# A build-time clock that orders a kernel's instructions gets measured durations and finer dependencies

## The chip, the cores and the metric

The kernel runs on one core of one Trainium2 chip. The metric is the device time of one execution in microseconds, the median of several runs; less is better. A core has TensorE (PE, with its weight loads as PEld), VectorE (DVE), ScalarE (ACT), GpSimd (POOL) and SyncE (SP, which here only issues DMAs). Each takes its instructions strictly in the order in which they stand in its queue, and semaphores order the engines among each other.

## What is computed

Two blocks in float32 on one sequence of 256 positions and 2048 channels, each with a modulation from a condition vector `c`, a mixer and a feed-forward part:

```
mod = silu(c) @ w_ada + b_ada
sh_m, sc_m, gt_m, sh_f, sc_f, gt_f = split(mod, 6)
h = rmsnorm(x) * (1 + sc_m) + sh_m
proj = h @ w_in
y = concat(hgrn2(proj), gated_delta(proj)) @ w_out     # block 1
x = x + gt_m * rmsnorm(y)
h = rmsnorm(x) * (1 + sc_f) + sh_f
y = square(relu(h @ w_ff1)) @ w_ff2                    # block 1
x = x + gt_f * rmsnorm(y)
```

The second block has the same frame; its mixer is four kinds of attention side by side (with a forgetting gate, "fox"; compressed, selected and windowed, "nsa"; dilated, "dil"; the difference of two softmaxes, "diff"), and its feed-forward part is a gated one, `(silu(u @ w_gate) * (u @ w_up)) @ w_down`. The gated delta rule solves a unit lower triangular system of 64 by 64 for each chunk and head:

```
m = where(strict, beta * (k @ k.T) * gamma, 0)
sol = triangular_solve(eye + m, [v * beta, k * beta * exp(g)])
```

## The kernel before

All weights stream once from HBM, 512 KB to a DMA on SP's queue, into a ring of `raw` buffers. A product keeps float32's precision by splitting: ScalarE copies a raw tile to a rounded high part (`wh<-raw`), VectorE or GpSimd subtracts to get the low part (`wl<-raw,wh`), and TensorE adds three products, x high with w high, x high with w low, x low with w high, into a PSUM bank `g`. The split activations are `hT`, and `rh`, `rl` or `o2h`, `o2l` further on. A split weight tile is called a unit here; there are four slots for `wh` and `wl`, sometimes six. The other large stream is that of the modulation weights (`ada`), which VectorE multiplies by a column of silu(c) and sums (`acc<-raw,csil,acc`); the sum over partitions of such an `acc` is then taken by TensorE, either as columns (`col_gen`, `mx<-c,acc`) or as a row (`row_gen`, which splits `acc` into `ah` and reads `mx<-ah,ones_r`).

Around the stream stand the mixers. Each piece of one is a Python generator (`hg_gen`, `gd_gen`, `fox_gen`, `nsa_gen`, `dil_gen`, `diff_gen`), a filler, which emits a few instructions at a time. `fill` is called between groups of weight products and decides, from a clock kept while the kernel is built (`_Clock`), whether a filler's next piece is due, whether the next weight unit is to be prepared (`late_prep`, `prep_at`), and which engine makes its low part (`l_eng`). Every instruction goes through `_Eng`, which emits it and tells `_Clock.run`; so nearly all instructions carry that helper's line, L169. The order in which the generators emit is the order in the engines' queues, and nothing reorders it later.

In one place fillers are forced. `run(b)`, at the start of a block of products, empties the list `pri` of evacuations down to one. The evacuation of the second half's first block (`ev_q`) waits until `hg_gen` of the first half has set `hg_done`, and while it waits `run` calls `fill_step(True)`:

```
def run(b):
    while len(pri) > 1:
        clk.end = 0.0
        pri_step()
        if not clk.end:
            fill_step(True)
```

A forced step takes the filler whose due time is the smallest, whichever that is. No weight product is emitted meanwhile. The gated-delta filler `gd_gen` inverts its triangular matrix there by doubling: six rounds, each of three groups of four small matmuls on TensorE with a copy by another engine behind each (`mx<-gdP,gdE`; `mx<-gdG,gdT`; and `mx<-c,gdP`, a transposition).

## Time and profile before

| what | value |
|---|---|
| time, median of 3 runs | 2801.25 us (2799.2 to 2802.51) |
| time of the profiled execution | 2811.73 us |
| its span, from the first to the last instruction | 2809.9 us |
| granted TensorE clock, mean over the span | 0.968 |
| TensorE busy | 2642.9 us, 94% |
| VectorE busy | 1842.7 us, 66% |
| ScalarE busy | 1283.6 us, 46% |
| GpSimd busy | 477.0 us, 17% |
| read from HBM | 636.27 MB, 228 GB/s over the span |

The profiled execution lasted 0.37% longer than the median of the unprofiled ones, and 1.8 us of it lie outside the span. Busy shares are means over stages with different limits; the stages are told apart by stretches of time. The granted clock is given as a share of full speed: 1.00 is 2.4 GHz, 0.50 is 1.2 GHz, and a value between them is a mean over both levels.

### The profile page before, as it was taken

The numbers are of one execution on the slowest core, as the hardware profiler recorded it, in microseconds if no ns is written. First come the engines' busy times: TensorE is split into PE (matmuls) and PEld (weight loads), VectorE is DVE, ScalarE is ACT, GpSimd is POOL, SyncE is SP. The second block draws the span as 40 slices with busy tenths as digits, with TensorE's granted clock in tenths as the row PEclk, the third lists the DMA queues.
The fourth block names the chain that finished last, engine by engine and source line by source line (L and its number), as shares of the span: only waits on it lengthen the run. The fifth ranks groups of instructions, "written<-read, shape, count | busy, mean of one in ns | idle before, by whom it ended". The sixth has DMA issues, their size and how long they took to land. (4 is left out here: it accounts for less than half of the span.)

```text
span 2809.9 us, 39852 instructions
## 1 busy us (share of the span) xinstructions
PE 2642.9 (94%) x15169; PEld 2244.2 (80%) x15169; DVE 1842.7 (66%) x2237; ACT 1283.6 (46%) x2148; POOL 477.0 (17%) x296
## 2 busy tenths in 40 slices
PE   7997889999889999999998899998879999999998
PEld 4887777868778787887886798886668888888887
DVE  3567957764577777777855546566777756564566
ACT  3433344344554454454454436454454544543443
POOL 1000141232120000000002474663620000000001
PEclk9999979999999999999999899999989999999999
DMA  9976858782658989989965674667747777665664
GB/s 361 310 258 229 226 145 244 225 248 91 202 195 274 313 282 300 315 275 318 303 199 168 179 216 151 218 223 238 242 157 239 237 243 237 193 189 191 191 189 144
DMA packets 399807, 643.61 MB, mean 229 GB/s; under 512 B 31480, under 2 KB 198088, under 8 KB 398208
## 3 DMA queue, kind: packets, MB, share of 16 engines
q1 hardware_dynamic: 396528, 628.26, 70.0%
q10 hardware_dynamic: 2336, 10.42, 1.0%
q8 instruction: 119, 1.95, 0.3%
q0 software_dynamic: 752, 2.39, 0.2%
q14 instruction: 72, 0.59, 0.1%
HBM read 636.27 MB, written 4.19 MB: 228 GB/s over the span
## 5 line engine op out<-in xcount | busy, mean ns | idle before, releaser
L169 ACT ACTIVATE wh<-raw 128x1024 fp32r<-128x1024 f32 (+2 forms) x817 | 846.2, 1044 | 877.3 <-PE g L169 452.4
L169 PE MATMUL g<-hT,wh 128*128 128x512 f32 (+1 forms) x4448 | 1219.2, 345 | 13.2 <-ACT wh L169 11.3
L169 DVE TENSOR_TENSOR wl<-raw,wh 128x1024 fp32r<-128x1024 f32 x697 | 872.6, 1259 | 522.0 <-ACT wh L169 512.4
L169 PE MATMUL g<-hT,wl 128*128 128x256 f32 x3376 | 955.5, 283 | 13.5 <-DVE wl L169 11.1
L169 PEld LDWEIGHTS g<-hT,wh 128*128 128x128 f32 x4448 | 773.6, 191 | 138.0 <-issue 23.5
L169 PEld LDWEIGHTS g<-hT,wl 128*128 128x128 f32 x3376 | 644.4, 191 | 17.4 <-DVE wl L169 13.0
L169 DVE SCALAR_TENSOR_TENSOR acc<-raw,csil,acc 128x1024 f32<-128x1024 f32 x276 | 384.6, 1394 | 79.2 <-DMA raw<-in_ada_w_dram 76.8
L169 PE MATMUL g<-wh,rh 128*128 128x512 f32 x864 | 341.3, 395 | 0.0
L169 PE MATMUL g<-wl,rh 128*128 128x512 f32 x864 | 340.2, 394 | 0.0
L169 PE MATMUL g<-wh,rl 128*128 128x512 f32 x864 | 340.2, 394 | 0.0
L169 POOL TENSOR_TENSOR wl<-raw,wh 128x1024 fp32r<-128x1024 f32 (+3 forms) x120 | 282.9, 2369 | 219.0 <-ACT wh L169 183.8
L169 POOL TENSOR_TENSOR y<-y,gw 128x512 f32<-128x512 f32 x22 | 32.0, 1473 | 1293.4 <-ACT sq L169 745.5
L169 PE MATMUL g<-wh,hT 128*128 128x512 f32 (+3 forms) x736 | 234.1, 386 | 17.0 <-ACT hT L169 13.3
L169 PEld LDWEIGHTS g<-wh,rl 128*128 128x128 f32 x864 | 163.3, 189 | 36.8
L169 PEld LDWEIGHTS g<-wh,rh 128*128 128x128 f32 x864 | 163.4, 189 | 35.9
L169 PEld LDWEIGHTS g<-wl,rh 128*128 128x128 f32 x864 | 163.5, 189 | 35.6
L169 PEld LDWEIGHTS g<-wh,hT 128*128 128x128 f32 x736 | 137.9, 195 | 48.9 <-ACT hT L169 16.3
L169 PE MATMUL g<-wl,hT 128*128 128x512 f32 (+3 forms) x368 | 139.1, 378 | 6.2 <-POOL wl L169 4.0
L169 PEld LDWEIGHTS g<-wl,hT 128*128 128x128 f32 x368 | 72.0, 196 | 17.7 <-POOL wl L169 5.2
L169 PE MATMUL ada<-raw,csil 128*32 128x512 f32 x384 | 64.6, 658 | 9.8 <-DMA raw<-in_w_ada_dram 8.1
L169 POOL TENSOR_TENSOR gdE<-gdM,mk 128x512 f32<-128x512 f32 x28 | 37.8, 1350 | 89.8 <-PE mx L169 69.6
L169 ACT ACTIVATE relu<-g 128x256 f32<-128x256 f32 (+1 forms) x62 | 22.2, 389 | 66.6 <-PE g L169 66.5
(447 smaller groups left out, 2519.0 us busy)
## 6 DMA issues: line engine op xcount, KB each, us to landing
raw<-in_w_ff_dram SPq DMA_DIRECT2D x256, 512.0 KB, 5.6
raw<-in_w_ada_dram SPq DMA_DIRECT2D x192, 512.0 KB, 5.9
raw<-in_ada_w_dram SPq DMA_DIRECT2D x192, 512.0 KB, 5.1
raw<-in_w_in_dram SPq DMA_DIRECT2D x176, 512.0 KB, 5.8
raw<-in_ffn_w_gate_dram SPq DMA_DIRECT2D x88, 512.0 KB, 4.5
raw<-in_ffn_w_up_dram SPq DMA_DIRECT2D x88, 512.0 KB, 4.6
raw<-in_ffn_w_down_dram SPq DMA_DIRECT2D x88, 512.0 KB, 4.4
raw<-in_w_out_dram SPq DMA_DIRECT2D x60, 512.0 KB, 4.7
```

Of the source, the lines that this page charges most:

```text
L169: r = f(out, *a, **kw)
```

## The change

`_Clock` tracked each buffer as a whole; it now tracks it in parts of 128 columns, and keeps apart when a part was read, when the buffer was last used at all, and when it becomes free for its next owner. The costs of operations get new constants. A VectorE operation with two SBUF inputs is charged more while a longer GpSimd `tensor_tensor` runs (`held_up`). And the sums of a modulation vector (`col_gen`, `row_gen`) are due 4.0 us after their `acc` was written, in place of 0.2; only the first vectors, which TensorE sums itself (`cg`), keep 0.2. No instruction is written or left out by hand: all that can change is the order in each queue and the engine that makes a low part.

```diff
@@ -77,8 +77,9 @@
 
     def __init__(s):
         s.t = {"pe": 0.0, "dve": 0.0, "act": 0.0, "pool": 0.0, "dma": 0.0, "qsync": 0.0, "qact": 0.0, "qpool": 0.0}
-        s.wr, s.rd, s.keys, s.count = {}, {}, {}, {}
+        s.wr, s.rd, s.keys, s.count, s.free, s.used = {}, {}, {}, {}, {}, {}
         s.end = 0.0
+        s.pool = (0.0, 0.0)
 
     def key(s, ap):
         t = ap.tensor
@@ -94,10 +95,21 @@
                 s.count[tag] = c + 1
                 k = (tag, c % bufs)
                 if n != k:
-                    f = max(s.rd.get(k, 0.0), s.wr.get(k, (0.0, ""))[0])
-                    s.rd[k] = f
+                    s.free[k] = s.used.get(k, 0.0)
             s.keys[n] = k
         return k
+
+    def parts(s, ap):
+
+        k = s.key(ap)
+        if ap.space == bass.MemoryType.DRAM:
+            return [(k, 0)]
+        o = ap.offset % ap.ap[0][0] if ap.ap[0][0] else ap.offset
+        e = sum((n - 1) * st for st, n in ap.ap[1:])
+        return [(k, c) for c in range(o // 128, (o + e) // 128 + 1)]
+
+    def written(s, ap):
+        return max(s.wr.get(p, (0.0, ""))[0] for p in s.parts(ap))
 
     def cost(s, eng, op, out, ins):
         n = 1
@@ -109,21 +121,31 @@
             if op == "transpose":
                 return max(n, 128) * 0.417e-3 * 2
             if ins[0].dtype == FR:
-                return n * 0.417e-3 * (1 if n >= 256 else 4) + 2.5e-3
-            return 4 * 0.417e-3 * max(n, 128)
+                return n * 0.417e-3 * (1 if n >= 256 else 4) + 13.5e-3
+            return 4 * 0.417e-3 * max(n, 128) + 10e-3
         if eng == "dve":
             if op == "tensor_scalar" and all(x.space != bass.MemoryType.PSUM for x in ins):
-                return n * 0.521e-3 + 0.07
-            return n * 1.042e-3 + 0.07 + (0.06 if op == "scalar_tensor_tensor" else 0.0)
+                return n * 0.521e-3 + 0.12
+            return n * 1.042e-3 + 0.1 + (0.04 if op == "scalar_tensor_tensor" else 0.0)
         if eng == "act":
-            return n * 0.833e-3 + 0.1
+            return n * 0.833e-3 + 0.16
         if op == "tensor_tensor":
-            return n * 2.2e-3 + 0.1
+            return max(n * 2.2e-3 + 0.1, 0.5)
         return n * 1.5e-3 + 0.1
 
+    def held_up(s, eng, op, start, d, ins):
+
+        if eng == "dve" and start < s.pool[1]:
+            n = sum(x.space != bass.MemoryType.PSUM and x.shape[-1] > 1 for x in ins)
+            if n > 1 or op == "tensor_scalar" and n:
+                over = min(d / 0.45, s.pool[1] - max(start, s.pool[0]))
+                if over > 0:
+                    return d + 0.55 * over
+        return d
+
     def run(s, eng, op, out, ins, accs):
-        outs = [s.key(o) for o in [out] + accs]
-        inks = [s.key(i) for i in ins]
+        outs = [p for o in [out] + accs for p in s.parts(o)]
+        inks = [p for i in ins for p in s.parts(i)]
         if op == "dma_start":
             n = 4
             for x in out.shape:
@@ -134,14 +156,17 @@
             q = eng
             d = s.cost(eng, op, out, ins)
             if accs:
-                d += 0.1
+                d += 0.17
         start = s.t[q]
         for k in inks + outs:
             w = s.wr.get(k)
             if w and not (op == "dma_start" and w[1][0] == "q" and k in outs):
                 start = max(start, w[0] + (0.0 if eng == "pe" == w[1] else 0.06 if w[1] == q else 0.13))
         for k in outs:
-            start = max(start, s.rd.get(k, 0.0))
+            start = max(start, s.rd.get(k, 0.0), s.free.get(k[0], 0.0))
+        d = s.held_up(eng, op, start, d, ins)
+        if eng == "pool" and op == "tensor_tensor" and d > 0.6:
+            s.pool = (start, start + d)
         if op == "dma_start":
             s.t[q] = start
             s.t["dma"] = max(s.t["dma"], start - 3.0) + d
@@ -152,6 +177,8 @@
             s.rd[k] = max(s.rd.get(k, 0.0), done)
         for k in outs:
             s.wr[k] = (done, q)
+        for k in outs + inks:
+            s.used[k[0]] = max(s.used.get(k[0], 0.0), done)
         if eng != "pe":
             s.end = max(s.end, done)
 
@@ -384,9 +411,9 @@
         if i >= len(items) or "raw" not in items[i]:
             return 0.0
         it = items[i]
-        at = clk.wr[clk.key(it["raw"])][0]
+        at = clk.written(it["raw"])
         if "ada" not in it and slots:
-            at = max([at] + [clk.rd.get(k, 0.0) for k in held.get(slots[0][0], ())])
+            at = max([at] + [clk.used.get(k, 0.0) for k in held.get(slots[0][0], ())])
         return at
 
     def prep_to(n):
@@ -786,7 +813,7 @@
         for vq in groups:
             def fin(vq=vq):
                 for v, q in vq:
-                    at = clk.wr[clk.key(accs[blk, v, q][0])][0] + 0.2
+                    at = clk.written(accs[blk, v, q][0]) + (0.2 if cg else 4.0)
                     urgent.append((at, col_gen(blk, v, q) if key is None else row_gen(blk, v, q, key, mul)))
             n = 8 if cg else 16
             for k in range(n):
```

The built programs hold 19911 instructions each, of the same kinds, and the DMAs on SP's queue stand in the same order. One low part of 128x576 more is made by GpSimd, and six units swap engines around it. Order differs in three stretches: in the first mixer (some 255 to 700 us of the trace of before), at single sums of the modulation up to 1460 us, and in the attentions (1680 to 2000 us). Elsewhere the queues read alike. The helper's line moves from L169 to L196.

The first place is TensorE's queue at the forced steps in the first mixer, from the last round that stood there before to the first products of the next block (`g` with `hT_176`). `gdP`, `gdG`, `gdT` and `gdE` are the matrices of the doubling, `gdM` the other pair of heads' matrix, `c_84` the constants. Before:

```order
L169 MATMUL mx<-gdP_3429,gdE_3430 128x64 x4
L169 MATMUL mx<-gdG_3425,gdT_3428 128x64 x4
L169 MATMUL mx<-c_84,gdP_3429 128x128 x4
L169 MATMUL mx<-gdP_3429,gdE_3430 128x64 x4
L169 MATMUL mx<-gdG_3425,gdT_3428 128x64 x4
L169 MATMUL g<-wh,hT_176 128x512
L169 MATMUL g<-wl,hT_176 128x512
L169 MATMUL g<-wh,hT_176 128x512 x2
L169 MATMUL g<-wl,hT_176 128x512
L169 MATMUL g<-wh,hT_176 128x512
L169 MATMUL mx<-c_84,gdP_3429 128x128 x4
L169 MATMUL mx<-gdP_3429,gdE_3430 128x64 x4
```

And of the changed kernel:

```order
L196 MATMUL mx<-gdG_3430,gdT_3433 128x64 x4
L196 MATMUL mx<-c_84,gdP_3434 128x128 x4
L196 MATMUL mx<-gdP_3434,gdE_3435 128x64 x4
L196 MATMUL mx<-gdG_3430,gdT_3433 128x64 x4
L196 MATMUL mx<-c_84,gdP_3434 128x128 x4
L196 MATMUL mx<-gdP_3434,gdE_3435 128x64 x4
L196 MATMUL mx<-gdE_3443,c_84 128x512
L196 MATMUL mx<-gdG_3430,gdT_3433 128x64 x4
L196 MATMUL mx<-zq,zk 128x128 x4
L196 MATMUL g<-wh,hT_176 128x512
L196 MATMUL g<-wl,hT_176 128x512
L196 MATMUL g<-wh,hT_176 128x512 x2
```

The fifth and sixth round (the last two pairs of `mx<-gdP,gdE` and `mx<-gdG,gdT`) stood behind the first products, spread among them; now they stand ahead of them, with the first steps of the other pair of heads (`gdM_3440`, `gdE_3443`, `zq,zk`).

The second place is ScalarE's queue at the diff heads, around the high part of the 533rd unit of the weights; `S_...` with `fd_...` are the exponentials of one head's scores and then their normalisation, `oq` an evacuation. Before, the unit is the last row but one, behind eight exponentials:

```order
L169 ACTIVATE S_17429,fd_17431<-S_17429,fd_17430 128x128
L169 ACTIVATE S_17429,fd_17431<-S_17429,fd_17430 128x256
L169 ACTIVATE S_17429,fd_17431<-S_17429,fd_17430 128x128
L169 ACTIVATE S_17429,fd_17431<-S_17429,fd_17430 128x256
L169 ACTIVATE wh<-raw 128x1024
L169 ACTIVATE oq_17154<-mx,cols 128x256
L169 ACTIVATE S_17478,fd_17480<-S_17478,fd_17479 128x128
L169 ACTIVATE S_17478,fd_17480<-S_17478,fd_17479 128x256
L169 ACTIVATE S_17478,fd_17480<-S_17478,fd_17479 128x128
L169 ACTIVATE S_17478,fd_17480<-S_17478,fd_17479 128x256
L169 ACTIVATE wh<-raw 128x1024
L169 ACTIVATE S_17429<-S_17429,fd_17432 128x128
```

And of the changed kernel, where it is the seventh row:

```order
L196 ACTIVATE oq_17154<-mx,cols 128x256
L196 ACTIVATE S_17444,fd_17446<-S_17444,fd_17445 128x128
L196 ACTIVATE S_17444,fd_17446<-S_17444,fd_17445 128x256
L196 ACTIVATE S_17444,fd_17446<-S_17444,fd_17445 128x128
L196 ACTIVATE S_17444,fd_17446<-S_17444,fd_17445 128x256
L196 ACTIVATE oq_17154<-mx,cols 128x256
L196 ACTIVATE wh<-raw 128x1024
L196 ACTIVATE S_17493,fd_17495<-S_17493,fd_17494 128x128
L196 ACTIVATE S_17493,fd_17495<-S_17493,fd_17494 128x256
L196 ACTIVATE S_17493,fd_17495<-S_17493,fd_17494 128x128
L196 ACTIVATE S_17493,fd_17495<-S_17493,fd_17494 128x256
L196 ACTIVATE wh<-raw 128x1024
```

The unit's high part (before, the first `wh<-raw` behind the exponentials of `S_17478`) stood behind the second head's four exponentials; now it stands ahead of them.

The third place is TensorE's queue where the last fox head's scores meet its values (`mx<-S,fv`). Before, among the products of a block of 256 columns whose inputs had long been there:

```order
L169 MATMUL g<-hT_12969,wh 128x256 x2
L169 MATMUL g<-hT_12969,wl 128x256
L169 MATMUL g<-hT_12969,wh 128x256 x2
L169 MATMUL g<-hT_12969,wl 128x256
L169 MATMUL mx<-S_15711,fv 64x256
L169 MATMUL mx<-S_15711,fv 64x128
L169 MATMUL mx<-S_15711,fv 64x256
L169 MATMUL mx<-S_15711,fv 64x128
L169 MATMUL g<-hT_12969,wh 128x256 x2
L169 MATMUL g<-hT_12969,wl 128x256
L169 MATMUL g<-hT_12969,wh 128x256 x2
```

And of the changed kernel, 96 products further on, in a block of 288 columns:

```order
L196 MATMUL g<-wl,hT_12969 128x288
L196 MATMUL g<-wh,hT_12969 128x288 x2
L196 MATMUL g<-wl,hT_12969 128x288
L196 MATMUL g<-wh,hT_12969 128x288
L196 MATMUL mx<-S_15816,fv 64x256
L196 MATMUL mx<-S_15816,fv 64x128
L196 MATMUL mx<-S_15816,fv 64x256
L196 MATMUL mx<-S_15816,fv 64x128
L196 MATMUL g<-wh,hT_12969 128x288
L196 MATMUL g<-wl,hT_12969 128x288
L196 MATMUL g<-wh,hT_12969 128x288 x2
```

The head's last matmuls moved from the first stretch into the next one.

## Rows read from the trace of the kernel before

**Rows 1.** Stretches: start:end, length, each engine's busy time (instructions), granted clock, DMA share, GB/s.

```profile
365.00:404.00 39.00, 25.99 (x124) 22.39 (x123) 13.56 (x28) 14.20 (x51) 17.92 (x17) 0.64 0.27 74
...
1690.00:1797.00 107.00, 105.45 (x851) 96.06 (x851) 66.53 (x103) 66.64 (x192) 56.26 (x24) 1.00 0.50 164
1797.00:1840.00 43.00, 39.01 (x274) 35.84 (x273) 25.79 (x29) 22.30 (x62) 29.00 (x18) 0.96 0.84 271
...
1905.00:2000.00 95.00, 81.16 (x355) 62.80 (x354) 73.65 (x90) 45.04 (x98) 34.55 (x19) 0.91 0.71 226
```

**Rows 2.** Timeline of TensorE, 364 to 412 us: start, length, operation, idle time before.

```profile
386.90 1.12 PE L169 MATMUL mx<-c,gdP 128*128 128x128 f32 x4 [0.58 <-DVE gdP L169]
387.81 1.81 PE L169 MATMUL mx<-gdP,gdE 128*128 128x64 f32 x8
...
398.44 1.12 PE L169 MATMUL mx<-c,gdP 128*128 128x128 f32 x4 [0.51 <-DVE gdP L169]
...
406.97 1.01 PE L169 MATMUL mx<-gdP,gdE 128*128 128x64 f32 x8
```

**Rows 3.** Timeline of GpSimd in the same stretch.

```profile
370.69 1.01 POOL L169 TENSOR_TENSOR rk<-rk,mhalf 128x4 f32<-128x4 f32 x1 [4.36 <-DVE rk L169]
...
373.04 1.04 POOL L169 TENSOR_TENSOR gdM<-c,gla 128x512 f32<-128x512 f32 x1
```

**Rows 4.** TensorE's waits by releaser, 245 to 365 us: total us, times, longest.

```profile
PE g L169 <- ACT wh L169: 9.8, 2, 6.5
```

**Rows 5.** ScalarE's longest wait, 274 to 300 us, in the same columns.

```profile
ACT zv L169 <- DVE part L169: 11.1, 1, 11.1
```

**Rows 6.** TensorE's waits, 404 to 460 us.

```profile
PE mx L169 <- DVE gdP L169: 3.1, 1, 3.1
PE mx L169 <- ACT gdG L169: 2.5, 1, 2.5
```

**Rows 7.** Timeline of TensorE at three sums of modulation vectors.

```profile
969.60 0.39 PE L169 MATMUL g<-wl,rh 128*128 128x512 f32 x1
969.83 0.39 PE L169 MATMUL g<-wh,rl 128*128 128x512 f32 x1
971.93 0.49 PE L169 MATMUL mx<-ah,ones_r 128*128 128x512 f32 x1 [1.72 <-ACT ah L169]
...
1115.52 0.66 PE L169 MATMUL mx<-c,acc 128*128 128x128 f32 x4 [2.88 <-DVE acc L169]
1329.53 1.12 PE L169 MATMUL mx<-c,acc 128*128 128x128 f32 x4 [3.30 <-DVE acc L169]
```

**Rows 8.** Timeline of VectorE near the first and the last of these.

```profile
973.14 0.75 DVE L169 TENSOR_SCALAR acc<-raw,csil 128x1024 f32<-128x1024 f32 x1
...
1324.73 1.28 DVE L169 TENSOR_TENSOR y<-g,y 128x512 f32<-128x512 f32 x2
```

**Rows 9.** Timeline of all engines, 1581 to 1587 us: units 430 and 431.

```profile
1582.90 1.22 DVE L169 TENSOR_TENSOR wl<-raw,wh 128x1024 fp32r<-128x1024 f32 x1
...
1583.89 2.46 POOL L169 TENSOR_TENSOR wl<-raw,wh 128x1024 fp32r<-128x1024 f32 x1 [10.52 <-DMA S<-in_nsa_cmp_w_dram]
...
1584.80 2.64 DVE L169 TENSOR_TENSOR wl<-raw,wh 128x1024 fp32r<-128x1024 f32 x1 [0.67 <-DMA raw<-in_w_in_dram]
```

**Rows 10.** Timeline of TensorE, 1683 to 1688 us, at a wait of the nsa scores.

```profile
1686.53 0.77 PE L169 MATMUL mx<-c,Sc 128*128 128x128 f32 x2 [1.00 <-DVE Sc L169]
```

**Rows 11.** TensorE's waits, 1797 to 1840 us.

```profile
PE g L169 <- POOL wl L169: 2.9, 4, 1.1
```

**Rows 12.** Timeline of TensorE at the diff heads, unit 533.

```profile
1968.35 0.79 PE L169 MATMUL g<-wh,o2h 128*128 128x512 f32 x1 [3.56 <-ACT wh L169]
1970.78 0.79 PE L169 MATMUL g<-wl,o2h 128*128 128x512 f32 x1 [1.64 <-POOL wl L169]
```

**Rows 13.** Timeline of ScalarE at the same place.

```profile
1967.26 1.04 ACT L169 ACTIVATE wh<-raw 128x1024 fp32r<-128x1024 f32 x1
```

**Rows 14.** TensorE's waits, 1905 to 2000 us.

```profile
PE mx L169 <- DVE on L169: 1.9, 1, 1.9
```

## The prediction, made before the changed kernel ran

> **What bounds the kernel now.** I read the table of stretches first, then TensorE's waits in the stretches that the change reorders, then the timelines at those waits. TensorE is busy for 2642.9 of 2809.9 us, so nearly every microsecond in which it isn't is a candidate, and nothing else is: the work of every engine stays the same, and only 167 us of idle time can shrink or grow. Three places hold what the new order touches.
>
> The first is the forced stretch of the first mixer, where in 39 us TensorE is busy for 26 at a granted clock of 0.64, so partly at 1.2 GHz [rows 1]. The reader is to see there the rounds of the doubling, one behind the other, with no product between them [rows 2]. The second is the sums of the modulation vectors, each of which can hold TensorE for up to 3.3 us [rows 7]. The third is the attentions: the stretch from 1690 to 1797 us is TensorE's (105.45 of 107 us busy, DMA share 0.50), the one after it has 4 us of idle time at a DMA share of 0.84, and that of the diff heads has 13.8 us of idle time in 95 [rows 1].
>
> **The forced stretch.** Before, four rounds of the doubling stood in it, now all six do, with the first steps of the other pair of heads.
>
> Two rounds lie between the transpositions at 386.90 and 398.44 us, so one takes (398.44 - 386.90) / 2 = 5.77 us [rows 2], and two more take +11.5. At full clock one would take less: a group of a round lasts 1.81 us there and 1.01 once products run again [rows 2], so with 0.8 off each of three groups a round takes 5.77 - 2.4 = 3.4, and two take 6.8. That is the low end; since nothing else is put beside the rounds, I take the high one.
>
> On GpSimd the other pair's `gdM` and `gdE` sweeps now stand ahead of the power `rk`, on which the rounds wait: 2 x 1.04 = +2.1 [rows 3]. Nothing would come of it if they fit in the 4.36 us for which GpSimd waited before `rk`; it is +4.2 if VectorE, which the same powers pass through, is late by as much again. I take 2.1. The other pair's own first matmuls add about 1, two 512-column groups at low clock, by the 1.12 of a group in the rows nearest to them [rows 2].
>
> The stretch may begin earlier. TensorE waited for ScalarE's high part for 9.8 us in all ahead of it, 6.5 in one wait [rows 4], while ScalarE stood 11.1 us at a `zv` step [rows 5] with that high part queued behind it; in the new order the step stands behind the unit. VectorE is busy nearly all that time, so most of the wait should turn into one for a low part. I take -2, with bounds 0 and -6.5.
>
> Given back behind the stretch: two rounds no longer stand among the products. A group of a round that stands between products takes about 1.01 [rows 2], six of them 6, and the matmuls of `hv,hf` and `hgA`, drawn ahead, about 1 by the same rows: -7. And TensorE's two waits for the other pair's chain, 3.1 + 2.5 = 5.6 [rows 6], come later in the products than the chain's new, earlier first steps require; half of them, -2.5, I count as gone, with bounds 0 and -5.6.
>
> Sum: 11.5 + 2.1 + 1 - 2 - 7 - 2.5 = +3.1. With the low ends about -8; with the high ones +9.7.
>
> **The sums of the modulation.** The due time moves their matmuls by a few products, at 0.23 us each (969.60 to 969.83 [rows 7]). At the first, 971.93 us, the low part `ah` now stands behind an `acc` step of 0.75 [rows 8] while its matmul stands six products earlier, 1.38: +2.1. At the second the matmul again stands six products earlier and still waits for the same `acc`: +1.4. At the third, the `acc` stands ahead of two additions of 1.28 us together [rows 8]: -1.3. Sum: +2.2. If the four microseconds do elsewhere what they are for in the clock, nothing is seen, since the other sums had no wait to lose. Bounds: -3.3 (the third wait gone) and +5.
>
> **Low parts that swap engines.** Unit 430, the first of a block that starts with nothing ahead, is made by GpSimd now: 2.46 in place of 1.22 us [rows 9], +1.2. The others lie where four slots of finished units cover them; without that cover each would cost the same 1.2.
>
> VectorE's low part that began at 1584.80 us, 0.91 into GpSimd's of 2.46, ended at 1587.44, 1.09 after GpSimd's end, and needs 1.22 alone [rows 9]: it got next to nothing done while GpSimd ran. The Trainium skill, in "SBUF — State Buffer", section "SBUF: two separate sides", says that a VectorE operation with two SBUF inputs and a GpSimd one that reads SBUF take the shared port pair as an exclusive lock for a whole instruction. The row agrees; by that rule the sum above would be the same.
>
> The new clock lets VectorE run on at 45% instead, which the row contradicts, so its finer costs are less true than they look; the second rival below rests on this row.
>
> **The attentions.** The last fox heads' matmuls move from the stretch where TensorE is the bound into the next one, where it waits 2.9 us for GpSimd's low parts [rows 11]. What moves costs as much time there as here unless it fills that wait, so the gain is at most -2.9, which I take since the moved groups outlast the four waits together; it is 0 if the waits stand ahead of them. The nsa wait of 1.00 [rows 10] should go, its matmuls being emitted later than their inputs by the new costs: -1.
>
> **The diff heads.** The 533rd unit's high part began only at 1967.26 us [rows 13], behind the four exponentials of the next head, and TensorE waited 3.56 for it and 1.64 for its low part [rows 12]. It now stands ahead of these exponentials, so both waits should go, and with the heads emitted more evenly the wait of 1.9 for `on` [rows 14] as well: -7.1. What is late next is the exponentials themselves, by one high part, 1.04 us [rows 13], ahead of VectorE's normalisation. Bounds: -9, if of the later waits some go too, and +2, if two heads meet.
>
> **Sum.** 3.1 + 2.2 + 1.2 - 2.9 - 1 - 7.1 = -4.5 us, against the profiled execution's 2811.73 us: 2807.2. That execution is 0.37% above the median of 2801.25, and I carry the difference over, not the ratio: 2796.7, rounded to 2796 for the few small waits that a better clock should spare elsewhere.
>
> **The rivals.** What a measurement of this kernel can tell from no change is about 0.2%, 5.6 us.
>
> First, the forced stretch costs in full, and the end is **slower**. Its place is the two rounds, its price the high ends: head 4.2, no earlier start, no wait of the other pair gone, hence 11.5 + 4.2 + 1 - 7 = +9.7, and the low clock lasting into the first products behind it, some eight products at 0.2 us more each, +2 (a group's 1.81 against 1.01 shows that ratio [rows 2]). It decides once the stretch outlasts 48 us. Then 2801.25 + 11.7 - 7.6 = 2805.4 with the other terms, and 2808 if the fox term is 0 as well. For it: no product is placed in the stretch to fill it. Against it: TensorE idled anyway ahead of it and behind it.
>
> Second, the change does not do what it says at the diff heads: VectorE's operations with two SBUF inputs stop for the whole of GpSimd's low parts, as in [rows 9], so the exponentials' normalisations come later by one low part and the wait only changes its name. The -7.1 becomes 0: +2.6, 2804. Against it: that row is at another place, and unit 533's low part was GpSimd's before too [rows 12].
>
> The Trainium skill's rule in "SBUF — State Buffer", "SBUF: two separate sides", speaks for this rival.
>
> Third, the gain is larger: the clock stays up in the rounds (6.8 in place of 11.5) and the products ahead of the stretch really lose the 6.5: -4.5 - 4.7 - 4.5 = -13.7, 2787. For it: TensorE would have more to do in the stretch than the 26 us in 39 it had. Against it: each group still waits for a copy.
>
> **How the numbers follow.** Forecast (-1 to -9 us): 0.42. First rival 0.20, second 0.19, third 0.19. The forecast's case lies on both sides of the bound of 5.6 us, a little more than half of it beyond: 0.23 faster and 0.19 within. With the third rival 0.42 faster; within 0.2% the 0.19, most of the second and a little of the first, 0.37; slower the rest, 0.21. The range reaches from 2784, the third rival with a little of the attentions' bounds, to 2809, the first with the fox term at 0; the forecast's own is 2792 to 2800.
>
> **What would show it.** In the changed kernel's profile, no product of TensorE between the `zk`, `zq` transpositions and the sixth round, some 44 to 50 us in place of 39; six `mx<-gdG,gdT` groups ahead of the first `g<-wh,hT`; no wait of over 2 us for `wh` near 1967 us; `acc` waits at the second sum of over 4 us. The prediction is wrong if the stretch is as long as before or 60 us long, if the diff heads' idle time is still 13 us, or if order elsewhere, which I costed at nothing (the two gated-delta halves behind 460 us), gains or loses more than 5 us.

## The result and the profile after

| | before | after |
|---|---|---|
| time, median | 2801.88 us (2799.2 to 2802.93, 4 runs) | 2819.39 us (2816.48 to 2824.33, 4 runs) |
| ratio after to before | | 1.0066, 95% interval 1.0048 to 1.0083 |
| span of the profiled execution | 2809.9 us | 2815.7 us |

The change makes the kernel slower by 0.66%, some 18 us. The profiled execution of before was 10 us longer than its median and that of after was not, so the two profiles lie only 5.8 us apart. Where a stage of before is compared below, the profiles of the experiments that kept its order in that stage are taken in.

Stretches of the profile after, in the columns of [rows 1]: the forced stretch of the first mixer, the stretch behind the nsa and fox heads, and the diff heads.

```profile
367.00:423.00 56.00, 36.65 (x175) 30.67 (x173) 15.48 (x32) 19.09 (x66) 25.39 (x22) 0.66 0.17 47
...
1790.00:1870.00 80.00, 71.45 (x507) 65.42 (x506) 49.06 (x83) 46.01 (x130) 41.88 (x23) 0.91 0.59 189
1905.00:2010.00 105.00, 94.04 (x415) 72.86 (x414) 78.47 (x93) 51.19 (x105) 47.14 (x22) 0.95 0.74 240
```

The forced stretch lasts from 367.47 to 422.93 us, 55.5 in place of 38.0 (365.46 to 403.42), with a DMA share of 0.17 and a mean granted clock of 0.66 in the row above. Timeline of TensorE in it, the rows that answer to [rows 2], with what it waited for first:

```profile
374.22 2.07 PE L196 MATMUL mx<-gdM,c 128*128 128x512 f32 x2 [5.71 <-POOL gdM L196]
...
385.85 1.12 PE L196 MATMUL mx<-c,gdT 128*128 128x128 f32 x4 [6.18 <-DVE gdT L196]
...
392.76 1.11 PE L196 MATMUL mx<-c,gdP 128*128 128x128 f32 x4 [0.59 <-DVE gdP L196]
...
400.32 1.11 PE L196 MATMUL mx<-c,gdP 128*128 128x128 f32 x4 [2.35 <-DVE gdP L196]
...
406.19 1.06 PE L196 MATMUL mx<-c,gdP 128*128 128x128 f32 x4
...
410.96 0.66 PE L196 MATMUL mx<-c,gdP 128*128 128x128 f32 x4 [0.52 <-DVE gdP L196]
...
416.13 1.11 PE L196 MATMUL mx<-c,gdP 128*128 128x128 f32 x4 [0.52 <-DVE gdP L196]
...
422.93 0.48 PE L196 MATMUL g<-wh,hT 128*128 128x512 f32 x1
```

The first round and the first product of before:

```profile
379.99 1.12 PE L169 MATMUL mx<-c,gdT 128*128 128x128 f32 x4 [7.51 <-DVE gdT L169]
...
403.42 0.77 PE L169 MATMUL g<-wh,hT 128*128 128x512 f32 x1
```

The five transpositions between six rounds are at 392.76 to 416.13, so four rounds took 23.37 us, 5.84 each; the first round begins 5.9 us later than before (385.85 against 379.99), and the first product comes at 422.93 against 403.42. GpSimd ahead of the rounds, and VectorE, on which its powers wait:

```profile
365.95 3.22 POOL L196 TENSOR_TENSOR ol<-hgA,oh 128x512 fp32r<-128x512 f32 x1 [10.13 <-ACT oh L196]
372.15 1.01 POOL L196 TENSOR_TENSOR rr<-rr,mhalf 128x4 f32<-128x4 f32 x1 [2.98 <-DVE rr L196]
...
377.12 1.01 POOL L196 TENSOR_TENSOR rk<-rk,mhalf 128x4 f32<-128x4 f32 x1
```

```profile
367.96 2.29 DVE L196 SCALAR_TENSOR_TENSOR acc<-raw,csil,acc 128x1024 f32<-128x1024 f32 x1
370.18 1.21 DVE L196 TENSOR_TENSOR wl<-raw,wh 128x1024 fp32r<-128x1024 f32 x1
371.31 0.68 DVE L196 SCALAR_TENSOR_TENSOR zv<-th,zv 128x512 f32<-128x512 f32 x1
371.91 0.15 DVE L196 TENSOR_SCALAR rr<-ss 128x4 f32<-128x4 f32 x1
```

The reader is to see a queue, not a slow engine: `rr` is a step of 0.15 us, but stands behind an addition (2.29 us beside GpSimd's `ol`, 1.28 alone), a low part and `zv`; GpSimd stands 2.98 us in front of its power, and everything that [rows 3] names, `gdM` and `rk`, comes behind it. Before, the same power was taken 12 us earlier:

```profile
360.34 3.11 POOL L169 TENSOR_TENSOR rr<-rr,mhalf 128x4 f32<-128x4 f32 x1 [3.44 <-DVE rr L169]
```

TensorE's waits ahead of the stretch and in it, 245 to 430 us, those behind it, 423 to 720 us, and those in the first block's feed-forward part, 840 to 1525 us:

```profile
PE g L196 <- DVE hv L196: 9.6, 1, 9.6
...
PE g L196 <- ACT wh L196: 0.2, 1, 0.2
```

```profile
PE mx L196 <- DVE zv L196: 4.5, 1, 4.5
...
PE g L196 <- DVE wl L196: 1.8, 1, 1.8
PE mx L196 <- ACT gdG L196: 1.4, 1, 1.4
...
PE mx L196 <- ACT gdP L196: 1.1, 1, 1.1
PE mx L196 <- DVE gdP L196: 0.7, 2, 0.5
```

```profile
PE mx L196 <- DVE ah L196: 2.0, 1, 2.0
PE mx L196 <- DVE acc L196: 1.2, 1, 1.2
```

The wait of [rows 4] for high parts went from 9.8 to 0.2, and one of 9.6 for `hv`, an evacuation on VectorE, stands in its place. The waits of [rows 6] have shrunk (3.1 for `gdP` on VectorE to 0.7). Those for `wl`, `gdG` and `gdP` on ScalarE, 4.4 us in all, fall between 430 and 448 us; before, TensorE did not wait at these products (404 to 431 us). The wait for `zv` has grown from 1.9 to 4.5. The waits for `acc` of [rows 7], 2.9 and 3.3, are down to one of 1.2.

Behind the fox heads, where [rows 11] showed 2.9 us of waits: VectorE, the GpSimd row beside it, and the matmul that waits behind them.

```profile
1827.87 3.31 DVE L196 SCALAR_TENSOR_TENSOR acc<-raw,csil,acc 128x1024 f32<-128x1024 f32 x1 [3.99 <-DMA raw<-in_ada_w_dram]
1831.10 2.36 DVE L196 TENSOR_TENSOR colt<-red,cols 128x4 f32<-128x4 f32 x1
1833.50 2.27 DVE L196 SCALAR_TENSOR_TENSOR Affn<-colt,cols 128x4 f32<-128x4 f32 x1
```

```profile
1830.37 5.38 POOL L196 TENSOR_TENSOR wl<-raw,wh 128x1024 fp32r<-128x1024 f32 x2 [0.28 <-ACT wh L196]
```

```profile
1839.86 3.43 PE L196 MATMUL mx<-kD,qC 64*128 64x128 f32 x12 [5.32 <-DVE S L196]
```

Two VectorE steps on 4 columns, 0.15 and 0.16 us elsewhere, took 2.36 and 2.27 beside GpSimd's low parts of 2.7 each; the scores `S` came 5.3 us late.

At the diff heads, 1905 to 2010 us, the answer to [rows 14]:

```profile
PE g L196 <- POOL wl L196: 5.7, 4, 1.9
PE mx L196 <- DVE v L196: 2.5, 1, 2.5
PE mx L196 <- DVE S L196: 1.8, 1, 1.8
```

The 3.6 for unit 533's high part is gone, the waits for `on` too; 2.5 for `v` are new and those for GpSimd's low parts grew from 3.1 to 5.7.

**Stage by stage.** Weight products stand in the same order in all kernels (12240 of them in each of the traces, in one sequence), so a stage can be cut by their number. This table is worked out from the start of the product with the first number to that with the second, for the profiles that have one or the other order there.

| products | stage | order of before: mean us (profiles, range) | changed order |
|---|---|---|---|
| 1200 to 1320 | forced stretch | 71.7 (8, 70.0 to 72.3) | 94.8 (2, 92.2 and 97.3) |
| 1320 to 2160 | rest of the first mixer | 243.5 (8, 240.5 to 246.5) | 243.2 (2, 242.7 and 243.6) |
| 2520 to 5900 | first feed-forward part | 689.2 (10, 683.6 to 694.2) | 680.4 (5, 679.0 to 681.9) |
| 6360 to 7320 | nsa and fox heads | 174.4 (12, 172.4 to 176.7) | 165.4 (5, 163.1 to 169.5) |
| 7320 to 7680 | behind them | 61.0 (12, 59.4 to 64.4) | 77.5 (4, 74.8 to 80.2) |
| 7680 to 8640 | dilated and diff heads | 265.3 (11, 262.8 to 269.7) | 261.2 (5, 258.6 to 267.8) |

### The profile page after: what moved, and what is told of

Same layout as the page of the kernel before. It is cut to its first block, busy times and chain, and to the rows that moved or that the text cites. A ratio compares the mean times of both kernels' runs of the same rounds, so it can differ in the third digit from the quotient of the medians.

```text
span 2815.7 us, 39871 instructions
## 1 busy us (share of the span) xinstructions
PE 2642.5 (94%) x15169; PEld 2245.3 (80%) x15169; DVE 1835.4 (65%) x2236; ACT 1284.5 (46%) x2148; POOL 478.2 (17%) x297
## 5 line engine op out<-in xcount | busy, mean ns | idle before, releaser
L196 ACT ACTIVATE wh<-raw 128x1024 fp32r<-128x1024 f32 (+2 forms) x817 | 845.8, 1044 | 900.6 <-PE g L196 440.7
L196 PE MATMUL g<-hT,wh 128*128 128x512 f32 (+1 forms) x4448 | 1215.6, 344 | 15.9 <-DVE hv L196 9.6
L196 DVE TENSOR_TENSOR wl<-raw,wh 128x1024 fp32r<-128x1024 f32 x696 | 869.6, 1257 | 541.7 <-ACT wh L196 533.0
L196 PE MATMUL g<-hT,wl 128*128 128x256 f32 x3376 | 953.9, 283 | 13.4 <-DVE wl L196 7.9
L196 PEld LDWEIGHTS g<-hT,wh 128*128 128x128 f32 x4448 | 772.4, 191 | 138.7 <-issue 33.3
L196 PEld LDWEIGHTS g<-hT,wl 128*128 128x128 f32 x3376 | 643.5, 191 | 16.3 <-DVE wl L196 8.7
L196 DVE SCALAR_TENSOR_TENSOR acc<-raw,csil,acc 128x1024 f32<-128x1024 f32 x276 | 394.9, 1431 | 80.7 <-DMA raw<-in_ada_w_dram 77.5
L196 PE MATMUL g<-wh,rh 128*128 128x512 f32 x864 | 339.1, 392 | 0.0
L196 PE MATMUL g<-wh,rl 128*128 128x512 f32 x864 | 338.9, 392 | 0.0
L196 PE MATMUL g<-wl,rh 128*128 128x512 f32 x864 | 338.7, 392 | 0.0
L196 POOL TENSOR_TENSOR wl<-raw,wh 128x1024 fp32r<-128x1024 f32 (+3 forms) x121 | 289.2, 2403 | 216.3 <-ACT wh L196 214.2
L196 PE MATMUL g<-wh,hT 128*128 128x512 f32 (+3 forms) x736 | 238.4, 392 | 15.6 <-ACT hT L196 11.9
L196 POOL TENSOR_TENSOR y<-y,gw 128x512 f32<-128x512 f32 x22 | 32.1, 1476 | 1282.0 <-ACT sq L196 735.4
L196 PEld LDWEIGHTS g<-wh,rl 128*128 128x128 f32 x864 | 162.3, 188 | 36.0
L196 PEld LDWEIGHTS g<-wh,rh 128*128 128x128 f32 x864 | 162.3, 188 | 36.0
L196 PEld LDWEIGHTS g<-wl,rh 128*128 128x128 f32 x864 | 162.4, 188 | 35.7
L196 PEld LDWEIGHTS g<-wh,hT 128*128 128x128 f32 x736 | 140.9, 198 | 48.7 <-ACT hT L196 15.1
L196 PE MATMUL g<-wl,hT 128*128 128x512 f32 (+3 forms) x368 | 140.6, 382 | 4.8 <-POOL wl L196 3.0
L196 PEld LDWEIGHTS g<-wl,hT 128*128 128x128 f32 x368 | 73.1, 199 | 15.3 <-POOL wl L196 3.7
L196 PE MATMUL ada<-raw,csil 128*32 128x512 f32 x384 | 63.7, 662 | 9.1 <-DMA raw<-in_w_ada_dram 7.4
L196 POOL TENSOR_TENSOR gdE<-gdM,mk 128x512 f32<-128x512 f32 x28 | 35.6, 1271 | 94.3 <-PE mx L196 74.2
L196 PE MATMUL mx<-c,y 128*128 128x128 f32 x96 | 20.8, 346 | 31.5 <-DVE y L196 25.6
```

The source lines that it names most:

```text
L196: r = f(out, *a, **kw)
```

## The experiments

Most run both clocks side by side, fed with the same instructions, and let one or the other answer, so that the change acts in one stage alone and the queues read as before in all others. At the border the due times of waiting fillers are shifted by the two clocks' difference.

```diff
+class _Dual:
+    def run(s, *a):
+        s.old.run(*a)
+        s.new.run(*a)
+    @property
+    def t(s):
+        return s.c.t
...
-    clk = _Clock()
+    clk = _Dual()
...
     drain(lambda: g.get("hg_done") == 1)
+    clk.use("old", fillers, urgent)
```

From E5 on, `use` is also given the due time of the sums. All ratios are to the kernel before; a figure in us is the ratio's distance from 1 times before's median of 2802 to 2805.

**E1, E2, E3: one stage each.** The border of E1 is the line above; E2 has the changed clock from there to the second mixer, E3 from there on.

> The changed clock orders only the first mixer; from its end on the clock of before does. Theory A (the loss is made by the forced stretch of the first mixer, where the two profiles lie 19 us apart behind it and 18 us apart at its end): 2801.9 + 18 = 2820 us, as slow as the changed kernel. Theory B (the loss is spread, and the attentions cost at least as much as the mixer): 2810 us or less.

> The changed clock, with the later due time of the sums, orders only the feed-forward part of the first block. The two profiles differ there by 14 us in favour of the change, in three steps of 4.7 us at the sums. If the steps belong to the order (theory A), 2801.9 - 14 = 2788 us. If they belong to the one profiled execution of before, which took 10 us longer than its median (theory B), 2802 us within 3.

> The changed clock orders only from the second block's mixer on. By the two profiles the attentions give and take (some 11 us gained early, 19 lost behind 1790 us, 7 gained at the diff heads), which sums to +1: 2803 us (theory A). Theory B, that they carry half of the loss: 2811 us.

Measured: E1 1.0070 (1.0047 to 1.0093), +20 us. E2 0.9966 (0.9952 to 0.9981), -9.5 us. E3 1.0017 (0.9999 to 1.0035), +4.8 us. The sum, +15, lies in the interval of the whole, +13 to +23. The loss is the first mixer's. The gain in the feed-forward part belongs to the order and not only to the one profiled execution of before. The attentions as a whole are not told from no change.

**E4: forced steps for the recurrent heads alone**, in the kernel before.

```diff
             if not clk.end:
-                fill_step(True)
+                hg = [f for f in fillers if f[1].gi_code.co_name == "hg_gen"]
+                if hg:
+                    rest = [f for f in fillers if f not in hg]
+                    fill_step(True, hg)
+                    fillers[:] = rest + hg
+                else:
+                    fill_step(True)
```

> The kernel before, but a forced step takes only the filler on which the stretch waits (the first half's recurrent heads), so none of the gated-delta rounds stands in it. Theory A (the rounds in the stretch are what it costs, 23 us for four of them, less what comes back when they stand among products, at most 3 us each): 2801.9 - 23 + 12 = 2791 us, range 2783 to 2797. Rival: the stretch lasts as long as the recurrent heads' own chain (power, scale, split, transposition), so nothing is gained and the rounds, now among the products, cost 3 us each: 2806 to 2814 us.

Measured: 2789.74 us, 0.9954 (0.9939 to 0.9969), -13 us. TensorE's timeline at the stretch:

```profile
365.98 1.12 PE L169 MATMUL mx<-c,hgA 128*128 128x128 f32 x4 [0.77 <-DVE hgA L169]
366.98 0.63 PE L169 MATMUL mx<-c,zk 128*128 128x128 f32 x4
369.11 0.80 PE L169 MATMUL g<-wh,hT 128*128 128x512 f32 x1 [1.49 <-ACT hq L169]
```

The product that came at 403.42 before comes at 369.11: what the stretch really waits for lasts 3 us. Between products 1200 and 1320 this profile has 38.3 us in place of 72.0, and 263.5 in place of 244.3 up to 2160, so of 33.7 us 19.2 are paid back where the rounds now stand. The same matmuls are cheaper there: by starts of TensorE's rows, with the idle time ahead of each taken off, those that are no products take 27.1 us less between products 1100 and 1320 (148 fewer) and 16.3 more from there to 2160 (148 more). Part of them stand in this stretch, in the columns of [rows 1]:

```profile
400.00:500.00 100.00, 94.64 (x672) 84.98 (x670) 70.16 (x98) 40.94 (x99) 30.34 (x20) 0.95 0.74 204
```

**E5, E15: the same edit under the changed clock**, in the first mixer alone (E5) and in the whole changed kernel (E15).

> As the run with the changed clock in the first mixer alone, but its forced steps take only the recurrent heads' filler, so the six gated-delta rounds leave the stretch. Theory A (the forced stretch carries the whole loss of 20 us): 2790 us, the time of the kernel before with the same edit. Theory B (a part of the loss lies elsewhere in the mixer: the late VectorE steps ahead of the stretch and the 6 us lost near 640 us): 2796 to 2804 us.

> The whole change, with forced steps that take only the recurrent heads' filler. By the parts measured one by one: -8.9 (first mixer with that edit), -10.4 (feed-forward), +5.4 (attentions) = 2803 - 14 = 2789 us. Rival: the forced stretch is not all that the change costs, and the time stays above that of the kernel before, 2803 us.

Measured: E5 2795.86 us, 0.9968 (0.9954 to 0.9982), -9 us; E15 2793.21 us, 0.9959 (0.9946 to 0.9972), -11.5 us. Taking the rounds out of the stretch turns +20 into -9 and +18 into -11.5, and E15's sum of the parts, -14, lies within its interval. The stretch of E5 ends 7.5 us later than that of E4, behind the same VectorE queue:

```profile
373.46 1.17 PE L324 MATMUL mx<-c,hgA 128*128 128x128 f32 x4 [5.45 <-DVE hgA L324]
376.62 0.80 PE L324 MATMUL g<-wh,hT 128*128 128x512 f32 x1 [1.98 <-ACT hq L324]
```

So theory B of E5 holds for a part: between E4 and E5 remain 4 us of time (intervals overlapping) and 7.5 us of lateness in the profile.

**E6, E7: how many rounds.** E6 has before's clock and the later due time, E7 the changed clock and the early one, both in the first mixer alone.

```diff
-        s.c = s.new
-        s.late = 4.0
+        s.c = s.old        # E6; E7: s.new
+        s.late = 4.0       # E7: 0.2
```

> The clock of before everywhere; only the due time of the modulation's sums is 4.0 in place of 0.2 us, and only in the first mixer. By the built order two and a half gated-delta rounds stand in the forced stretch in place of four. Theory A (time follows the number of rounds in the stretch, some 5 us net for each by the run with six): 2801.9 - 1.5 x 5 = 2794 us. Theory B (the later sums are themselves what costs, and the rounds only came with them): 2806 us or more.

> The changed clock (durations, parts, GpSimd's hold-up) in the first mixer alone, but with the sums due after 0.2 us as before. By the built order three and a half rounds stand in the stretch. Theory A (number of rounds): 2801.9 - 0.5 x 5 = 2799 us. Theory B (the measured durations themselves make a worse order): 2812 us or more.

Measured: E6 2798.70 us, 0.9982 (0.9967 to 0.9997), -5 us; E7 2804.86 us, 0.9999 (0.9984 to 1.0013), 0. Neither part of the change costs anything by itself; together they put six rounds in the stretch. In the built orders the number is 2.5 for the due time alone, 3.5 for the clock with the early sums, 4 before, 6 with both. The time follows this number in its order, not in proportion: E6's and E7's stretches end at 399.92 and 404.64 us, with their first round at 384.73 and 385.39, as late as in the changed kernel.

**E8, E12: the gains together.** E8 is E4 with the changed clock in the feed-forward part, E12 has it at the diff heads too.

> The clock of before with forced steps for the recurrent heads alone, and the changed clock in the first block's feed-forward part. If the two gains of 12.2 and 10.4 us are independent: 2801.9 - 22.6 = 2779 us. Rival: the gain in the feed-forward part is a better start out of the mixer and is had only once: 2788 us.

> Forced steps for the recurrent heads alone, the changed clock in the feed-forward part and, without the later due time, at the diff heads, that of before elsewhere. If the gains of 12.2, 10.4 and 7 us are independent: 2802 - 29.6 = 2772 us. Rival: the diff heads give nothing: 2780 us, as with the first two alone.

Measured: E8 2780.81 us, 0.9913 (0.9898 to 0.9928), -24 us: the two gains add up. E12 2774.63 us, 0.9906 (0.9883 to 0.9930), -26 us: the third is not told from nothing. Both beat both kernels.

**E9, E10: the attentions in two.** E9 switches to the changed clock at the dilated heads, E10 switches back there.

```diff
         st["p"] += 1
+        if st["p"] == 850:
+            clk.use("new", 0.2, fillers, urgent)
```

> The clock of before up to the dilated heads, the changed one from there on, with the sums' due time of before: of what the change moves only the diff heads' order is left. The prediction's term of -7.1 us (the two waits for unit 533 and the one for the normalised output gone): 2802 - 7 = 2795 us. Rival: the waits only change their names: 2802 us within 3.

> The changed clock from the second mixer's start to the dilated heads, that of before on either side: nsa and fox order as changed, diff heads as before. If the fox matmuls that move behind 1790 us cost more there than they free ahead of it (theory A, by the two profiles -11 and +18): 2802 + 8 = 2810 us. The prediction's terms for this stretch (-2.9 for fox, -1 for nsa, +1.2 for unit 430): 2799 us.

Measured: E9 0.9996 (0.9981 to 1.0012), -1 us; E10 1.0033 (1.0012 to 1.0054), +9 us; together +8, within E3's interval (0 to +10). TensorE's waits of E9 at the diff heads, 1870 to 2015 us:

```profile
PE g L324 <- POOL wl L324: 5.7, 4, 1.9
PE mx L324 <- DVE S L324: 4.5, 1, 4.5
PE mx L324 <- DVE v L324: 3.1, 1, 3.1
```

The wait for unit 533's high part is gone here as in the changed kernel, and the time is not. Of the five profiles with this order at these heads four are 5 to 7 us shorter than the mean of before and this one is 2.5 us longer; by time E9 gains at most 5 us.

E10 has the profiles' picture: from product 6360 to 7320, 9.9 us of matmuls other than products have left and the idle time has grown by 1.1; from 7320 to 7680, 10.5 us of them have come and the idle time has grown by 2.0. What moved cost as much in the second stretch as in the first. Over both stretches the four profiles with the changed order take 241.8 us (239.8 to 243.9) and the twelve with that of before 235.4 (231.8 to 238.5); of the 6.4 us between them 5.1 are idle time, for the greater part waits for `S` (7.0 us in E10, 2.7 before). By time E10 loses 3 to 15 us, so the two agree.

**E11, E13: due time or durations in the feed-forward part.**

> The clock of before everywhere; only the sums' due time is 4.0 in place of 0.2 us, and only in the first block's feed-forward part. Theory A (the gain of 10.4 us there is the due time's: a sum that is read later no longer waits for its last addition): 2802 - 9 = 2793 us. Theory B (the measured durations place the sums better): 2800 us or more.

> The changed clock in the first block's feed-forward part alone, but with the sums due after 0.2 us as before. If the due time carries the gain (theory A): 2803 us within 3. If the measured durations and the finer parts carry it (theory B): 2794 us.

Measured: E11 0.9987 (0.9971 to 1.0003), -3.6 us; E13 0.9982 (0.9969 to 0.9994), -5 us. Neither theory: the two parts seem to carry about half each of E2's -9.5. The waits from 840 to 1525 us say more for the due time. E11's only ones at a sum, then E13's only one:

```profile
PE mx L324 <- DVE ah L324: 2.3, 2, 2.0
```

```profile
PE mx L324 <- DVE acc L324: 5.5, 2, 3.3
```

With the later due time the waits for `acc` are gone or short under either clock (at most 1.2 us, in the changed kernel), with the early one they stay. By the profiles E11's stage has 681.5 us, close to the range with the whole change, and E13's 687.3, as before. The timed runs don't bear that out, and the split stays open.

**E14: the low parts behind the fox heads on VectorE**, otherwise E10.

```diff
+        if st["p"] in (819, 821, 822, 824):
+            return dve
```

> As the run with the changed clock for nsa and fox alone (+9.3 us), but four low parts of 128x1024 behind 1822 us are made by VectorE in place of GpSimd, so the column sums, the additions and the scores of the dilated heads find no GpSimd low part beside them. If VectorE's standing behind GpSimd is what costs there (two steps of 0.16 us took 2.2 each, additions of 1.28 up to 3.4): 2813 - 5 = 2808 us, and the wait for S gone. If only the moved matmuls cost: 2813 us or, with 4 x 1.2 us more on VectorE, above.

Measured: 1.0025 (1.0010 to 1.0040), +7 us, not told from E10. VectorE's small steps, and TensorE's waits from 1790 to 1850 us:

```profile
1818.43 0.15 DVE L324 TENSOR_TENSOR colt<-red,cols 128x4 f32<-128x4 f32 x1
1818.62 0.16 DVE L324 SCALAR_TENSOR_TENSOR Affn<-colt,cols 128x4 f32<-128x4 f32 x1
```

```profile
PE g L324 <- ACT wh L324: 3.6, 1, 3.6
...
PE mx L324 <- DVE S L324: 1.4, 1, 1.4
```

That VectorE stood behind GpSimd is shown: with no low part beside them the steps are back at 0.16 us, and the wait for `S` falls from E10's 3.0 to 1.4. That this was the loss is not: a wait of 3.6 for a high part took its place, and the two stretches together last 242.9 us, as long as with the changed order.

## Why the prediction was wrong, point by point

**The forced stretch, +3.1, was mis-sized: it measured +20** (E1), and that alone turned the sign. That two more rounds stand in it with nothing beside them was right, and the first rival had it too, with +11.7 at most; neither price was large enough. Between the two profiles the start of product 2160 moves by +18.7 us. By the prediction's terms:

- Two more rounds and the other pair's first matmuls, 11.5 + 1 = +12.5: the first round to the first product took 37.08 us (385.85 to 422.93) against 23.43 (379.99 to 403.42), +13.6. About right, though two groups at the row's 1.12 make 2.2 and not 1.
- "The stretch may begin earlier", -2, and the head, +2.1, together +0.1: the first round began 5.9 us later. This is the first step that failed. The wait for the high part went as expected, but one for `hv` on VectorE stood in its place, and the last product ahead of the stretch starts no earlier (365.33 before, 365.57 after). Twenty matmuls (of `hgA`, `hv,hf` and `hv,hgA`), which the working took to be drawn ahead from behind the stretch, came from products 900 to 1200 instead, and sixteen of them now stand between that product and the stretch, whose start is 2.0 us later. The other 3.9 come with the late `rr`: the working had looked at ScalarE's queue, where the `zv` step moved out of the way, and took GpSimd's two more sweeps as the price of the head; it left out that VectorE's share of the same chain (`zv`, then `rr`) had come to stand behind an addition and a low part.
- "Given back", -7 and -2.5, together -9.5: 0.8 came back. This is the second step that failed, and the larger one. Work that leaves a place was counted as time gained, and the order of all that stays there as worth nothing. From the first product behind the stretch to product 1320 there are 36 fewer matmuls other than products, which take 5.0 us less; but 4.4 us of waits (`wl`, `gdG`, `gdP`) came where there were none, so this part lasts 27.3 us against 27.4. From there to product 1500 the change saves 6.8 us, 4.5 of them waits of the other pair's chain, more than the -2.5 counted; from 1500 to 2160 it loses 6.0, 3.8 of them waits, that for `zv` first. Products 1320 to 2160 together last as long as before, in the table's means too (243.2 against 243.5).

The low end of this sum, "about -8", comes to -11.3 by the bounds stated with its terms (6.8 + 0 + 1 - 6.5 - 7 - 5.6); no other number uses it. The first rival's condition, a stretch of more than 48 us, was met with 55.5, but the low clock that it saw last into the first products did not: they take 0.39 us each from 423.24, against 0.63 from 403.99 before.

**The sums, +2.2, were wrong in sign: -9.5** (E2). The step counted how many products a matmul moves, against the wait that it met in one execution. What a later due time does is take the matmul away from an `acc` that is only just written. And a wait costs more than itself: behind the one of 2.88 us at 1115.52 the products start some 0.43 us apart in place of 0.23 from about 1117 to 1120.35. The granted clock was at the lower of its two levels, 1.2 GHz, behind each of the three waits of [rows 7]; these are stretches of before, in the columns of [rows 1]:

```profile
973.60:977.00 3.40, 3.40 (x9) 2.64 (x8) 3.40 (x5) 1.63 (x2) 0.00 (x0) 0.50 0.93 296
1117.00:1120.40 3.40, 3.40 (x12) 2.73 (x11) 3.05 (x4) 2.81 (x14) 0.00 (x0) 0.51 1.03 374
1328.60:1335.40 6.80, 5.87 (x18) 4.90 (x19) 3.99 (x4) 4.45 (x19) 0.00 (x0) 0.50 0.99 338
```

And the whole stage of the changed kernel:

```profile
840.00:1525.00 685.00, 681.73 (x3446) 576.94 (x3445) 522.21 (x539) 326.63 (x483) 8.70 (x8) 1.00 0.86 284
```

In the changed kernel's profile the idle time from product 2520 to 5900 is 6.0 us less (3.3 in place of 9.3) and the products themselves take 4.6 us less. The prediction named as its bound "the third wait gone"; the three waits shrank together, and the stretches of low clock behind them went.

**The fox heads, -2.9, and the nsa wait, -1: +9 with unit 430's +1.2** (E10; no run has that unit alone). The condition was stated (the gain is 0 if what moves doesn't fill the wait), the wrong side of it taken, and no loss allowed for. What moved cost the same there, and the stretch's own waits grew, the one for `S` from 0.9 to 3.0 (E10) and 5.3 (after). The Trainium skill's rule ("SBUF — State Buffer", section "SBUF: two separate sides"), by which a VectorE operation with two SBUF inputs and a GpSimd operation that reads SBUF hold a shared port pair one after the other for a whole instruction, is borne out by these rows (0.16 us became 2.27 beside a low part of 2.7, and 0.16 again without it in E14). It names the wait, not the loss, as E14 shows: without these low parts the time is the same, so what the loss comes from, beyond the longer waits, stays open.

**The diff heads, -7.1: -1 by time** (E9, -5 to +3). The two waits for unit 533 went as predicted, and in E9's profile their time came back as waits for `v`, for `S` and for GpSimd's low parts. This is the second rival's number, which was given only 0.19, but not its mechanism. The normalisations do not stand behind GpSimd's low parts in the new order: VectorE takes 0.88 to 0.90 us for each pair of them in E9 and in the changed kernel. It was before the change that one pair took longer; the third of four pairs before, then in E9:

```profile
1968.63 2.64 DVE L169 SCALAR_TENSOR_TENSOR S<-S,fd 128x128 f32<-128x128 f32 x2 [1.24 <-ACT S L169]
```

```profile
1964.53 0.88 DVE L324 SCALAR_TENSOR_TENSOR S<-S,fd 128x128 f32<-128x128 f32 x2 [0.27 <-ACT S L324]
```

Since four other profiles with this order are 5 to 7 us shorter at these heads, a gain of up to 5 us stays possible.

**The order elsewhere, costed at nothing**, lost 6.0 us from product 1500 to 2160 (497 to 675 us before), more than the 5 that the prediction named as a sign of being wrong; the `zv` wait behind 640 us, 2.6 us more, is its largest piece. Of the other signs, the six groups ahead of the first product and the missing wait for `wh` near 1967 us came, the `acc` wait of over 4 us did not, and the stretch outlasted the 44 to 50 us named.

## What to carry to other kernels

A place where a scheduler is forced to emit something should force only what it waits for: here that one edit was worth 13 us, more than the finer model. A change of a planner's numbers should be read first at such places, where nothing overlaps, by counting what comes to stand in them on every queue on which the chain inside depends. What leaves a crowded place gives its time back only if nothing that stays there waits in its stead. A change like this should be measured stage by stage, since the whole hides a loss of 20 us and a gain of 10 behind one ratio.

## What was not expected

A wait of 3 us for an `acc` was followed by 3.4 us of low clock, in which the products behind it took nearly twice as long (the starts 0.43 us apart named above). Products 2520 to 5900 spread over 10.6 us in ten profiles with the order of before, and over 2.9 us in five with the changed one, under which such waits were short: in the ten the clock stood at 1.2 GHz for 0 to 13.7 us of this stage, in the five it never did.

The same small matmuls cost 27.1 us in the forced stretch and 16.3 among the products (E4), although they then stood in the way of products. The granted clock was 0.64 in the stretch and 0.95 where many of them went (the row in E4's paragraph); that the clock is all of the difference isn't shown.
